# Input projection of a hybrid encoder block: direct products replaced by Strassen's scheme over column pairs

## The chip, the cores and the metric

The kernel runs on 1 core of one Trainium2 chip. The metric is device time in microseconds (us); a profiled execution also gives the span from its first to its last instruction.

## The reference

One encoder layer over 2048 tokens of width 1024, batch 1, float32. What matters here is its first part:

```
h = rmsnorm(x, norm1_g)                     # 2048 x 1024
proj = h @ w_in                             # 1024 x 3264 columns
hq, hi, hf_fwd, hf_bwd, hg = 5 x 512 columns   # recurrence head group
c_q, c_kv, k_r = 384, 256, 64 columns          # latent attention group
y_a = (gla(silu(hq), hi, hf_fwd) + reversed gla(silu(hq), hi, hf_bwd)) normed * silu(hg)
y_b = attention(rmsnorm(c_q) @ w_q_b, rmsnorm(c_kv) @ w_kv_b, rope(k_r))
x = x + concat(y_a, y_b) @ w_out;  x = x + swiglu_ffn(rmsnorm(x));  rmsnorm(x)
```

`gla` is a gated linear recurrence over chunks of 64 tokens, 8 heads of 64; it runs forward in time once and backward in time once.

## The kernel before

Every large product is done in three passes (`mm3`, L191 to L195): each operand is split into a rounded high part and the rest, and high x high, high x low and low x high are summed in PSUM. So each operand tile costs one copy that rounds (often ScalarE) and one subtraction (VectorE or GpSimd). The FFN already works by Strassen's scheme (`slots`, `prods`, `after`); the input projection doesn't.

The part before attention has three stages.

- Stage A (L317 to L367). Token blocks of 512 are normed and transposed (`x_block`); blocks 1 to 3 are prepared as a side channel while products run. Then come the gate columns `hg` (feature-major, `feat_tile`, 128 weights columns against 512 tokens), `hi` as `tp_v` (token-major, 256 columns), `c_q` as `tp_cq` (384) and `c_kv` with `k_r` as `tp_ckv` (320), normed in place and stored.
- Stage B (L586 to L621). For each pair of heads p = 0 to 3 and each block b = 0 to 3, three feature tiles `fp_q`, `fp_f`, `fp_b`, then the elementwise part (`sigmoids`, `decays`: Sigmoid, Ln, scan, Exp) and, as the side channel `ch_f`, the forward part of the recurrence (`rec_block`). The reverse recurrence of p (`back_block`, channel `ch_b`, then `head_norm`) starts when its four blocks are done.
- Stage C (L656 to L788). Latent inputs are loaded back, transposed on TensorE and split (`latent_block`), and projected to keys, values and queries (`tok_proj`, `head_proj`); what is left of the reverse recurrence runs beside it.

Each engine executes its instructions in the order in which they stand; that order comes from the tile framework's scheduler, which keeps near the order of writing. The ticks (`tick`, one after each mm3 of 512 columns) say how far a side channel has got when the next product is written.

## Time and profile before

| | us |
|---|---|
| median of 3 runs | 3129.3 (3118.62 to 3129.41) |
| profiled execution, its own time | 3131.85 |
| its span | 3130.1 |
| TensorE busy in the span | 2985.8 (95%) |
| VectorE, ScalarE, GpSimd busy | 1920.2, 1256.7, 1210.5 |
| stage A, first load to first `fp_q` weights | 0 to 350.6 |
| stage B, to the end of the last `fp_b` | 350.6 to 789.3 |
| stage C, to the first attention scores | 789.3 to 964.8 |

Busy time is the union of an engine's instructions. TensorE's matmuls overlap in the pipeline, so what one costs is read from the distance between starts, and not from its duration. The granted clock was 0.986 of full speed over the span.

### The profile page before, as it was taken

The page shows a single profiled execution, that of the slowest core. Times are in us where ns is not written, and L with a number is a line of the kernel's source. Part 1 is how long each engine was busy: PE and PEld are TensorE (multiplying, and loading weights), DVE is VectorE, ACT ScalarE, POOL GpSimd, SP SyncE. Part 2 cuts the span into 40 slices and gives each one's busy share as a digit, 9 for nine tenths or more (in the row PEclk, how much of TensorE's full clock was granted, in tenths as well). Part 3 has the DMA queues.
Part 4 walks back from the last instruction along what each step waited for, and adds up shares of the span by engine and source line. Part 5 has one row for each costly group of instructions (what it writes and reads, how often), then busy time and mean ns, then how long its engine had stood idle before and what let it go on. Part 6 is the DMA issues. An engine that isn't in the chain of part 4 may idle for free.

```text
span 3130.1 us, 45080 instructions
## 1 busy us (share of the span) xinstructions
PE 2985.8 (95%) x16377; PEld 2491.0 (80%) x16377; DVE 1920.2 (61%) x3986; ACT 1256.7 (40%) x2365; POOL 1210.5 (39%) x1042
## 2 busy tenths in 40 slices
PE   7999999999789999999999999999899999999988
PEld 6899877777677888888877778888688887877776
DVE  6116557787686888888889865555755554432326
ACT  5101366656324555555633333333433333332233
POOL 1110132332333021211023466666566664365652
PEclk9999999999899999999999999999999999999999
DMA  5221112222553010100267543333533332764554
GB/s 178 71 64 57 61 60 83 80 85 81 184 187 131 21 48 28 46 25 19 71 197 227 182 141 100 104 103 101 163 103 101 101 101 100 244 204 139 165 158 154
DMA packets 313758, 349.66 MB, mean 112 GB/s; under 512 B 21016, under 2 KB 221248, under 8 KB 313536
## 3 DMA queue, kind: packets, MB, share of 16 engines
q1 hardware_dynamic: 307840, 339.68, 33.8%
q0 software_dynamic: 4608, 4.20, 0.5%
q8 instruction: 129, 2.11, 0.3%
q10 hardware_dynamic: 1088, 2.90, 0.3%
q14 instruction: 93, 0.76, 0.1%
HBM read 225.07 MB, written 121.63 MB: 111 GB/s over the span
## 4 chain that ended last, share of the span: by engine, by line
PE 58%; DVE 6%; DMA 6%; POOL 3%; issue 2%; ACT 2%; SPq 0%; DVEq 0%; ACTq 0%; POOLq 0%
PE pb L194 4%; PE pb L193 4%; PE pb L195 4%; PE t L885 3%; PE pc L194 2%; PE pa L193 2%; PE pc L195 2%; PE pa L194 2%; PE pa L195 2%; PE pc L193 2%; PE pd_P L194 2%; PE pd_P L195 2%; PE pd_P L193 2%; PE s L852 2%; PE o L193 2%
## 5 line engine op out<-in xcount | busy, mean ns | idle before, releaser
L198 ACT ACTIVATE pth<-t 128x512 fp32r<-128x512 f32 x256 | 153.5, 602 | 250.3 <-PE t L885 250.3
L1264 DVE TENSOR_TENSOR gl_P<-gr_P,gh_P 128x1024 fp32r<-128x1024 f32 x66 | 95.9, 1454 | 239.3 <-ACT gh_P L1263 239.3
L194 PE MATMUL pd_P<-dl_P,gh_P 128*128 128x512 f32 x528 | 208.8, 395 | 16.6 <-POOL dl_P L1255 16.6
L193 PE MATMUL pd_P<-dh_P,gh_P 128*128 128x512 f32 x528 | 207.2, 392 | 5.3 <-DVE t1d L1326 4.1
L859 DVE TENSOR_REDUCE mx<-s 128x1 f32<-128x512 f32 x256 | 175.1, 685 | 56.3 <-PE s L852 56.0
L195 PE MATMUL pd_P<-dh_P,gl_P 128*128 128x512 f32 x528 | 207.5, 393 | 0.0
L868 ACT ACTIVATE pr<-s,nb 128x512 f32<-128x512 f32 x256 | 172.7, 689 | 14.8 <-DVE nb L862 10.9
L199 DVE TENSOR_TENSOR ptl<-t,pth 128x512 fp32r<-128x512 f32 x256 | 174.8, 684 | 2.8 <-ACT pth L198 0.5
L193 PE MATMUL o<-pth,vh 128*128 128x256 f32 x512 | 164.8, 322 | 0.3 <-DVE nb L862 0.3
L885 PEld LDWEIGHTS t<-ident,pr 128*128 128x128 f32 x1024 | 126.5, 141 | 40.5 <-DVE pr L875 1.8
L885 PE MATMUL t<-ident,pr 128*128 128x128 f32 x1024 | 153.9, 273 | 4.4 <-DVE pr L875 3.0
L1263 ACT ACTIVATE gh_P<-gr_P 128x1024 fp32r<-128x1024 f32 x66 | 69.8, 1058 | 203.7 <-PE pd_P L194 181.7
L651 POOL CAST qh<-qraw 128x256 fp32r<-128x256 f32 x31 | 12.4, 400 | 352.7 <-PE s L849 352.6
L195 PE MATMUL o<-pth,vl 128*128 128x256 f32 x512 | 144.0, 281 | 0.0
L194 PE MATMUL o<-ptl,vh 128*128 128x256 f32 x512 | 143.9, 281 | 0.0
L194 PEld LDWEIGHTS pd_P<-dl_P,gh_P 128*128 128x128 f32 x528 | 100.1, 190 | 41.6 <-POOL dl_P L1255 20.7
L1073 DVE TENSOR_TENSOR t<-t,pb 128x512 f32<-128x512 f32 x44 | 30.3, 688 | 162.8 <-PE pb L195 162.8
L875 DVE TENSOR_SCALAR pr<-pr,ri 128x512 f32<-128x512 f32 x256 | 127.7, 513 | 2.2
L193 PEld LDWEIGHTS pd_P<-dh_P,gh_P 128*128 128x128 f32 x528 | 100.3, 190 | 27.1 <-DVE t1d L1326 4.5
L487 POOL TENSOR_TENSOR Am<-az 64x128 f32<-64x128 f32 x64 | 44.1, 690 | 195.5 <-DVE az L484 171.7
L195 PEld LDWEIGHTS pd_P<-dh_P,gl_P 128*128 128x128 f32 x528 | 100.3, 190 | 20.6
L1069 DVE TENSOR_TENSOR U<-t,pb 128x512 f32<-128x512 f32 x44 | 30.2, 686 | 134.2 <-PE pb L195 134.2
(483 smaller groups left out, 9969.2 us busy)
## 6 DMA issues: line engine op xcount, KB each, us to landing
s_gA<-g SPq DMA_DIRECT2D x66, 256.0 KB, 3.2
s_gS<-gS SPq DMA_DIRECT2D x66, 256.0 KB, 2.0
gr_P<-s_gA SPq DMA_DIRECT2D x33, 512.0 KB, 4.2
gr_P<-s_gS SPq DMA_DIRECT2D x33, 512.0 KB, 4.6
B11r<-in_w_gate_dram SPq DMA_DIRECT2D x44, 256.0 KB, 3.9
B12r<-in_w_up_dram SPq DMA_DIRECT2D x44, 256.0 KB, 2.9
B22r<-in_w_up_dram SPq DMA_DIRECT2D x44, 256.0 KB, 2.9
B21r<-in_w_gate_dram SPq DMA_DIRECT2D x44, 256.0 KB, 3.2
```

The lines of the kernel that those rows point to most:

```text
L193: PE.matmul(ps, a_hi, b_hi, start=first, stop=False, skip_group_check=more)
L194: PE.matmul(ps, a_hi, b_lo, start=False, stop=False, skip_group_check=more)
L195: PE.matmul(ps, a_lo, b_hi, start=False, stop=last, skip_group_check=more)
L198: ACT.activation(hi, ps, AF.Copy)
L199: DVE.tensor_tensor(lo, ps, fr(hi), op=ALU.subtract)
L852: PE.matmul(ps, rq[:, qs], rk_lo[b], start=False, stop=True)
L859: last_mx[0] = DVE.tensor_reduce(mx[:, b:b + 1], ps, op=ALU.max, axis=AX.X)
L868: ACT.activation(PR[i][:, b, :], SB[i][b], AF.Exp, scale=SCALE, bias=nb, accum_out=rs[:, b:b + 1])
L875: DVE.tensor_scalar(PR[i][:, b, :], PR[i][:, b, :], ri, None, op0=ALU.mult)
L885: PE.transpose(ps[:, j, :], PR[i][:, b, j * P:(j + 1) * P], ident)
L1263: ACT.activation(hi, raw, AF.Copy)
L1264: DVE.tensor_tensor(lo, raw, fr(hi), op=ALU.subtract)
```

## The change

Everything up to the latent projections is rewritten; attention, output projection and FFN keep their instructions.

- Columns are taken in pairs of 128 (`COLS`): (forward gate, backward gate) and (query, output gate) for each p, three pairs of latent columns (the last pair overlaps, 768 columns for 704), and one pair of 256 for `hi`. Tokens are taken 1024 at a time (two "halves"), rows of w_in in halves of 512. A pair, half and product is 12 matmuls of 512 columns (48 of 256 for `hi`), with 7 products P1 to P7 in place of 8.
- The seven activation operands of half 0 are made on the way in (`x_even`, `x_odd`); those of half 1 are stored to DRAM and split when an operand of half 0 has had its last use (`stage`, `unstage`).
- The sums of weights T1 to T4 are made once by GpSimd and stored to DRAM (`w_sums`); each weight unit is loaded and split for each half anew (`b_load`, `b_make`).
- Products are combined by VectorE (`sums`), and a ScalarE copy takes P1 from PSUM.
- The order is: latent columns and `hi` of half 0, gates and queries of half 0, `hi` of half 1, gates and queries of half 1, latent columns of half 1. The reverse recurrence of p starts when its last block of half 1 is there, beside the remaining products; its scaling of the state moves from VectorE to ScalarE.
- SiLU replaces Sigmoid and a multiplication for `hq` and `hg`.
- Latent inputs are stored feature-major. They are normed after loading: squares, column sums on TensorE, and a product that spreads the factors over partitions; 20 groups of 4 transposes go, 4 groups for `k_r` come.

```diff
-        w = [load_w(wp, w_in[0, :, 2048 + p * P:2176 + p * P], P, f"hg{p}", 3, 4) for p in range(3)]
...
+    main = [(k, p) for p in range(4) for k in ("FB", "QH")]
...
+    islots = [(0, *s) for s in (
+        [(c, pr) for c in (c0, c1, c2) for pr in ("P1", "P2")]
+        + [(c0, "P6"), (c0, "P5"), (c0, "P7"), (c1, "P6"), (c0, "P4"), (c1, "P5"), (c0, "P3"), (c1, "P7"),
...
+        + chain(main)[:-2])]
...
+    islots += [(1, *s) for s in chain(main + [c0, c1, c2])]
...
+    def b_make(m):
+
+        while len(BU) < len(ulist) and len(BU) < ufirst[m] + RING:
+            j = len(BU)
+            if j == len(RAW):
+                b_load(True)
+            BU[j] = hi, lo = [w1.tile([P, 512], F32R, tag=f"w{c}", name=f"w{c}_{j}", bufs=RING) for c in "hl"]
+            ACT.activation(hi, RAW[j], AF.Copy)
+            (DVE if j % 7 in (1, 3, 5) else POOL).tensor_tensor(lo, RAW[j], fr(hi), op=ALU.subtract)
...
+    def x_odd(hf, xs):
+        yield from x_norm(2 * hf + 1, xs)
+        for j in range(4):
+            at = {}
+            for nm, k in (("A21", j), ("A22", j + 4)):
+                ps, g = x_turn(2 * hf + 1, k, xs)
...
+                ACT.activation(at[nm], ps, AF.Copy, scale=g)
...
+            POOL.tensor_tensor(at["S1"], at["A21"], at["A22"], op=ALU.add)
+            DVE.tensor_tensor(at["S3"], A1[j], at["A21"], op=ALU.subtract)
+            POOL.tensor_tensor(at["S2"], at["S1"], A1[j], op=ALU.subtract)
+            POOL.tensor_tensor(at["S4"], A1[j + 4], at["S2"], op=ALU.subtract)
+            if hf == 0:
+                for nm in ("A22", "S3", "S1", "S2", "S4"):
+                    hi, lo = hop[nm]
+                    ACT.activation(hi[:, j, :], at[nm], AF.Copy)
+                    DVE.tensor_tensor(lo[:, j, :], at[nm], fr(hi[:, j, :]), op=ALU.subtract)
...
+            for k in range(4):
+                mm3(ibank[c, key], wu[0][0][:, k, :], wu[0][1][:, k, :], ah[:, k, :], al[:, k, :],
+                    new and k == 0, k == 3, not new)
+                tick()
+            after1(hf, key, pr)
...
+    def sums(get, pr, a, b, c, t1, u2, u3):
+
+        if pr == "P1":
+            ACT.activation(get(t1), a(), AF.Copy)
+        elif pr == "P2":
+            return "C11", a()
+        elif pr == "P6":
+            DVE.tensor_add(get(u2), TM[t1], b())
+        elif pr == "P7":
+            DVE.tensor_add(get(u3), TM[t1], b())
+            DVE.tensor_add(TM[u3], TM[u3], c())
...
+            if d == "F":
+                DVE.tensor_scalar(o[hs, hs], tprev[hs, :], a_in[hs, :], None, op0=ALU.mult)
+            else:
+                ACT.activation(o[hs, hs], tprev[hs, :], AF.Copy, scale=a_in[hs, :])
...
-                for k in range(kt):
-                    ps = rec_tile(f"c{nm}T_{b}_{k}")
-                    for t in range(4):
-                        PE.transpose(ps[:, t * P:(t + 1) * P], src[:, t, k * P:(k + 1) * P], ident)
-                    split_psum(hi[:, k, :], lo[:, k, :], ps)
+                for t in range(4):
+                    PE.matmul(ps[:, t, :], sq[:, k0, t * P:(t + 1) * P], sum1[:, 0:2], start=True, stop=True)
+                r = rstd_of(ps[:, :, 0], 4, dim, f"rc{nm}_{b}")
...
+                R = rec_tile(f"cr{nm}_{b}")
+                PE.matmul(R, sum1, sq[:, k0 + 1, :], start=True, stop=True)
```

The change moves instructions in two places that matter below. The first is TensorE at the start of the program. Before, after the first transposes (`xT`) of token block 0, the products of the gate columns (`fp_hg`) take block 0's operands (`hh_194`, `hl_195`):

```order
L193 MATMUL fp_hg0_0_367<-hh0_194,wh_hg0_0_337 128x512
L193 MATMUL fp_hg1_0_432<-hh0_194,wh_hg1_0_347 128x512
L193 MATMUL fp_hg2_0_517<-hh0_194,wh_hg2_0_357 128x512
L304 MATMUL xT_0_4_301<-ident_74,x_0_0_58 128x128
L304 MATMUL xT_0_4_301<-ident_74,x_0_1_60 128x128
L304 MATMUL xT_0_4_301<-ident_74,x_0_2_62 128x128
L304 MATMUL xT_0_4_301<-ident_74,x_0_3_64 128x128
L194 MATMUL fp_hg0_0_367<-hl0_195,wh_hg0_0_337 128x512
L195 MATMUL fp_hg0_0_367<-hh0_194,wl_hg0_0_338 128x512
```

In the changed kernel six products (P1, P2 of three latent pairs) take block 0's operands; this is the end of them, and what follows:

```order
L201 MATMUL iP1c2_0_721<-hA11h_0_199,wh_4_499 128x512
L202 MATMUL iP1c2_0_721<-hA11l_0_200,wh_4_499 128x512
L203 MATMUL iP1c2_0_721<-hA11h_0_199,wl_4_500 128x512
L201 MATMUL iP6c0_0_817<-hS2h_0_201,wh_6_669 128x512
L201 MATMUL iP5c0_0_870<-hS1h_0_205,wh_7_713 128x512
L202 MATMUL iP5c0_0_870<-hS1l_0_206,wh_7_713 128x512
L203 MATMUL iP5c0_0_870<-hS1h_0_205,wl_7_714 128x512
L202 MATMUL iP6c0_0_817<-hS2l_0_202,wh_6_669 128x512
```

From the fourth of these rows on each product takes an operand (S2, S1) that is made of token blocks 0 and 1.

The second place is ScalarE in the middle of the gate and query products. Before, for p = 1, block 0 (L614 Sigmoid for the query, L401 and L402 Sigmoid for a gate, L410 Ln, L437 and L431 Exp, L485 and L486 copies of the recurrence, L206 an evacuation):

```order
L614 ACT_TABLE_LOAD
L614 ACTIVATE q_1_0_4501<-fp_q1_0_4446 128x512
L206 ACTIVATE kts_0_3_1_4551<-kt_0_3_1_4546 128x512
L401 ACTIVATE A0_1_0_4562<-fp_f1_0_4504 128x512
L402 ACTIVATE N0_1_0_4563<-fp_f1_0_4504 128x512
L410 ACT_TABLE_LOAD
L410 ACTIVATE A0_1_0_4562<-A0_1_0_4562,lb_78,oml_79 128x512
L485 ACTIVATE Am_0_3_0_4582<-G_0_3_0_0_4583 64x2x64
L486 ACTIVATE Am_0_3_0_4582<-G_0_3_0_0_4583 64x2x64
L437 ACT_TABLE_LOAD
L437 ACTIVATE al0_1_4440<-tot0_1_0_4658 128x8
L431 ACTIVATE A0_1_0_4562<-C0_1_0_4657 128x512
```

In the changed kernel, for p = 2 of half 1 (L594 and L596 Sigmoid, L691 Ln, L714 Exp, L667 scaling of the reverse state of p = 0, L358 rounding of a weight unit, L831 squares of the reverse part, L214 an evacuation):

```order
L594 ACT_TABLE_LOAD
L594 ACTIVATE N0_2_2_6151<-iP1FB2_1_5856 128x512
L596 ACTIVATE FB2P2_1_6153<-iP1FB2_1_5856 128x512
L667 ACTIVATE bdB1_1847<-T_B0_8_6169,al1_0_1858 64x64 x2
L691 ACT_TABLE_LOAD
L691 ACTIVATE FB2P2_1_6153<-FB2P2_1_6153,lb_77,oml_78 128x512
L831 ACTIVATE po_0_2_6045<-bo_0_2_5978 128x512
L358 ACTIVATE wh_140_6194<-wr_140_6056 128x512
L214 ACTIVATE kts_1_3_0_6216<-kt_1_3_0_6211 128x512
L667 ACTIVATE bdB0_1846<-T_B0_7_6240,al1_0_1858 64x64 x2
L358 ACTIVATE wh_141_6253<-wr_141_6103 128x512
```

Weight units and the scaling of the reverse state have come between the functions, and each function's table is still loaded anew: over the whole program ScalarE has 130 table loads for 98.

## Rows read from the trace of the kernel before

**Rows 1.** Busy time by stage; columns as named.

```profile
core 0: us, PE busy (x) PEld busy (x) DVE busy (x) ACT busy (x) POOL busy (x), PEclk, DMA share, GB/s
0.00:350.60 350.60, 326.48 (x2049) 304.12 (x2050) 154.18 (x567) 73.66 (x163) 36.60 (x36) 1.00 0.28 89
350.60:789.30 438.70, 422.75 (x3142) 334.09 (x3142) 299.17 (x786) 280.48 (x444) 143.86 (x178) 0.99 0.24 76
789.30:964.80 175.50, 145.75 (x875) 119.60 (x874) 120.56 (x300) 51.40 (x92) 56.42 (x70) 0.91 0.58 202
```

**Rows 2.** Tiles of stage A: duration ns min/median/max, first and last start.

```profile
L193 PE MATMUL fp_hg<-hh,wh_hg x128: 387/389/796, 22.1 to 125.5; 128*128 128x512 f32 x128
...
L193 PE MATMUL tp_v<-wh_v,hh x256: 278/283/284, 126.2 to 218.0; 128*128 128x256 f32 x128
...
L193 PE MATMUL tp_cq<-wh_cq,hh x128: 334/334/339, 218.4 to 285.0; 128*128 128x384 f32 x128
...
L193 PE MATMUL tp_ckv<-wh_ckv,hh x128: 306/309/468, 285.5 to 346.0; 128*128 128x320 f32 x128
```

**Rows 3.** Longest waits of TensorE in stage C: total, times, longest.

```profile
PE ckvT L682 <- DMA ckv<-s_ckv: 5.7, 2, 5.5
PE cqT L682 <- DVE ckvl L199: 5.4, 1, 5.4
```

**Rows 4.** Busy time in two windows of 50 us (stage C, FFN); columns as Rows 1.

```profile
850.00:900.00 50.00, 41.12 (x227) 32.48 (x226) 44.05 (x141) 12.47 (x21) 9.52 (x13) 0.97 0.73 247
1900.00:1950.00 50.00, 50.00 (x219) 40.67 (x218) 22.86 (x27) 15.42 (x27) 30.58 (x22) 1.00 0.33 103
```

**Rows 5.** Timeline of TensorE in stage C: start, duration.

```profile
942.24 0.60 PE L706 MATMUL qrT<-ident,qd 128*128 128x128 f32 x4
942.60 0.48 PE L193 MATMUL kn<-ckvh,wkh 128*128 128x512 f32 x1
```

**Rows 6.** The first transposes and ScalarE reading them; columns as Rows 2.

```profile
L304 PE MATMUL xT<-ident,x x128: 270/273/477, 10.5 to 82.5; 128*128 128x128 f32 x128
L306 ACT ACTIVATE hh<-xT,gcols x32: 679/688/707, 21.4 to 82.9; 128x512 fp32r<-128x512 f32 x32
```

**Rows 7.** Groups of the FFN's Strassen products, 1570 to 3130 us.

```profile
L1076 DVE TENSOR_TENSOR g<-t,U 128x512 f32<-128x512 f32 x44 | 73.2, 1664 | 5.4 <-ACT t L1074 0.7 <-DMA B11d_P<-in_w_down_dram 0.7
...
L1006 POOL TENSOR_TENSOR T<-B12r,B11r 128x512 f32<-128x512 f32 x44 | 57.7, 1312 | 95.4 <-DVE T4l L1022 92.6 <-DMA B12r<-in_w_up_dram 2.6
...
L1022 DVE TENSOR_TENSOR T4l<-T,T4h 128x512 fp32r<-128x512 f32 x44 | 31.2, 709 | 1.9 <-ACT T4h L1020 1.9
...
L1069 DVE TENSOR_TENSOR U<-t,pb 128x512 f32<-128x512 f32 x44 | 30.2, 686 | 134.2 <-PE pb L195 134.2
...
L1020 ACT ACTIVATE B11h<-B11r 128x512 fp32r<-128x512 f32 x44 | 27.8, 632 | 92.9 <-PE pa L194 82.0 <-DMA B11r<-in_w_gate_dram 7.3 <-PE pa L195 2.4
...
L1060 ACT ACTIVATE t<-pa 128x512 f32<-128x512 f32 x44 | 25.5, 579 | 0.2 <-PE pa L195 0.2
```

**Rows 8.** Groups on ScalarE, stage B: count, busy us, mean ns, idle before.

```profile
L410 ACT ACT_TABLE_LOAD x31 | 39.8, 1283 | 0.5
L437 ACT ACT_TABLE_LOAD x31 | 39.8, 1283 | 0.5
...
L401 ACT ACT_TABLE_LOAD x16 | 20.5, 1283 | 0.3
...
L614 ACT ACT_TABLE_LOAD x15 | 19.2, 1283 | 8.2 <-PE fp_q L195 8.1
```

**Rows 9.** Timeline of ScalarE in stage B, around a table load.

```profile
785.75 0.27 ACT L486 ACTIVATE Am<-G 64x128 f32<-64x128 f32 x1
786.04 1.28 ACT L437 ACT_TABLE_LOAD   x1
787.34 0.21 ACT L437 ACTIVATE al<-tot 128x8 f32<-128x8 f32 x1
```

**Rows 10.** Groups on VectorE, stage B.

```profile
L391 DVE TENSOR_SCALAR bdB<-T_B,al 64x64 f32<-64x64 f32 x80 | 28.0, 350 | 4.2 <-PE po L528 3.0
...
L615 DVE TENSOR_TENSOR q<-q,fp_q 128x512 f32<-128x512 f32 x16 | 10.9, 684 | 11.7 <-ACT q L614 11.7
```

More of the change, by code (lines that the diff above doesn't have):

```diff
@@ L96, in drain, with until @@
             tick()
+    def until(pred, *cs):
+        while not pred():
+            assert any(c.queue for c in cs)
+            for c in cs:
+                if c.queue:
+                    c.queue[0][1] = min(c.queue[0][1], clock[0])
+                    c.step()
     def fr(ap):
@@ new lines, in block_kernel, with b_load @@
+    ch_w, ch_f, ch_d, ch_b, ch_n, side = (Channel() for _ in range(6))
+    ulist = [(m, u) for m, (hf, key, pr) in enumerate(islots) for u in range(units(key))]
+    ufirst = {}
+    for j, (m, u) in enumerate(ulist):
+        ufirst.setdefault(m, j)
+    RAW, BU = {}, {}
+    RING, RAWS = 4, 3
+    def b_load(force=False):
+        j = len(RAW)
+        if j >= len(ulist):
+            return False
+        m, u = ulist[j]
+        hf, key, pr = islots[m]
+        nm = B_OF[pr]
+        if nm[0] == "T" and (key, u) not in summed:
+            if not force:
+                return False
+            until(lambda: (key, u) in summed, ch_w)
+        raw = RAW[j] = w1.tile([P, 512], F32, tag="raw", name=f"wr_{j}", bufs=RAWS)
+        if nm[0] == "T":
+            SP.dma_start(out=raw, in_=T_d[nm, key, u])
+        else:
+            SP.dma_start(out=b_view(key, raw), in_=b_src(key, nm, u))
+        return True
@@ new lines, in x_rest, with stage @@
+    def x_rest(xs1):
+        yield from x_odd(0, xs1)
+        for b in (2, 3):
+            xs = x_load(b)
+            yield 4
+            yield from (x_odd if b % 2 else x_even)(1, xs)
+    ibank, TM, decayed, done = {}, {}, set(), set()
+    staged = []
+    order2 = ["A11", "A12", "S2", "S1", "S3", "A22", "S4"]
+    def stage(m):
+        if order2:
+            i = order2.pop(0)
+            raws = [ws_b(j, f"hs_{i}_{j}") for j in range(4)]
+            for j in range(4):
+                SP.dma_start(out=raws[j], in_=h1_d[i][:, j, :])
+            staged.append((m, i, raws))
@@ new lines, in unstage, with hop_switch @@
+    def unstage(m):
+        _, i, raws = staged.pop()
+        hop_tiles(i, 1)
+        hi, lo = hop[i]
+        for j in range(4):
+            ACT.activation(hi[:, j, :], raws[j], AF.Copy)
+            DVE.tensor_tensor(lo[:, j, :], raws[j], fr(hi[:, j, :]), op=ALU.subtract)
+        stage(m)
+    def hop_switch(m):
+        if m == last_use["A11"] - 3:
+            until(lambda: not ch_w.queue, ch_w)
+            stage(m)
+        elif staged and last_use[staged[0][1]] <= m and m >= staged[0][0] + 2:
+            unstage(m)
@@ new lines, in block_kernel, with ws_a @@
+    es_a = ctx.enter_context(ExitStack())
+    stg = es_a.enter_context(pool("stg1"))
+    for _ in range(RAWS):
+        b_load()
+    def ws_a(s, nm):
+        return xpool.tile([P, 512], F32, tag=f"ws{s}", name=nm)
+    first_w = w_sums(c0, 0, ws_a)
+    next(first_w)
+    xs1 = x_load(1)
+    for _ in x_even(0, xs0):
+        pass
+    for _ in first_w:
+        pass
+    for key, u in ((c1, 0), (c2, 0), (v, 0), (v, 1)) + tuple((k, 0) for k in main[:2]):
+        ch_w.add(w_sums(key, u, ws_a))
@@ L369, in block_kernel @@
+    side.add(x_rest(xs1))
+    m1 = 0
+    while islots[m1][1][0] in "cv" or islots[m1][1] not in main:
+        product1(m1)
+        m1 += 1
+    drain(side, ch_w)
+    es_a.close()
     es_x.close()
+    rb = es_b.enter_context(pool("rb", side="right"))
     rec = es_r.enter_context(pool("rec", side="right"))
-    wp = es_l.enter_context(pool("w1b"))
+    tri = rb.tile([P, 2, 2, 64], U8, tag="tri", name="tri")
+    trif = rec.tile([P, 4, P], F32, tag="vb", name="trif", bufs=1)[:, 0:2, :].rearrange("p a (b n) -> p a b n", b=2)
@@ L427, in decays @@
             qk.append((A, C))
+            yield 1
         for d in range(2):
```

561 lines of the change are left out of this document (340 added, 221 removed).

## The prediction

> **What bounds the kernel now.** I read the stages first, since all changed work lies ahead of the first attention scores at 964.8 us. In stages A and B TensorE is busy 326 of 351 us and 423 of 439, while VectorE has 68% and ScalarE 64% of stage B; in stage C TensorE has only 146 of 175.5 [rows 1]. So A and B last as long as TensorE's work, with some 40 us of idle time between them, half of it before the first product at 22.1 us [rows 2]. Stage C also waits: for a reload from DRAM and for the first split operands, 11 us in its two longest waits [rows 3]. Where VectorE is busiest (88% of 50 us, in stage C) TensorE falls to 82% [rows 4]: this is what it looks like when helpers set the pace, though the latent reload plays a part there too.
>
> **The products.** Prices go by the distance of starts. In the FFN window 50 us hold 219 matmuls of 512 columns, 0.228 us each [rows 4]. The 768 matmuls of `tp_v` (256 of each pass) fill the time from 126.2 us to the first of `tp_cq` at 218.4, 0.120 us each; `tp_cq` then lasts to 285.5 (67.1 us) and `tp_ckv` to some 346.5 (61 us) [rows 2]. Before: 384 (`hg`) + 1152 (stage B) matmuls of 512 columns are 350 us, with 92 + 67 + 61 for the others 570 us. After, as the order has them: 11 pairs x 2 halves x 7 products x 12 = 1848 of 512 columns, 421 us, and 672 of 256, 81 us: 502 us. So 68 us of TensorE's work goes.
>
> **Latent operands on TensorE.** 20 groups of four transposes go and 4 come; a group takes 0.36 us (942.24 to 942.60) [rows 5], so 5.8 us goes. What comes is 32 matmuls with 2 columns and 8 with 512 columns of plain f32, neither in the trace at that shape: the first cost from 0 to 0.18 us each (two f32 transposes), the second from 0.23 [rows 4] to 0.72 (twice a group of transposes). That is 2 to 12 us; I take 10, a net of +4 us.
>
> **Stage A after.** To the first product 22 us as before [rows 2], since block 0 goes the same way. Then 252 matmuls of 512 (57.5 us) and 336 of 256 (40.3), the rest of the transposes (24 groups, 8.6), and small waits of 8 (before there were 12: 350.6 - 22.1, less 88 of `hg`, 92, 67, 61 and 8.6). New is a hole. Only the first six products (72 matmuls, 16.4 us) live on block 0; the order shows S1 and S2 right behind. For these, block 1 is normed, transposed and split on ScalarE in four steps of 2 copies at 0.688 [rows 6] and 5 at 0.632 [rows 7], 18 us, with four steps of three GpSimd sums at 1.31 [rows 7] in the same chain. It starts when block 0 is nearly done, so some 18 + 6 us of chain stand against 16 us of products, of which part is spent waiting for block 0 itself. The hole is 0 if the steps interleave perfectly and 24 us if nothing hides it; I take 15, since each step frees a quarter of a product only. Sum: 22 + 57.5 + 40.3 + 8.6 + 8 + 15 = 152 us.
>
> **Stage B after (gates, queries, `hi` of half 1, latent columns of half 1).** TensorE: 1596 matmuls of 512 (1344 + 252), 364 us, 336 of 256, 40 us, and the recurrence's own matmuls, which before were 422.75 - 1152 x 0.228 = 160 us [rows 1]: 564 us.
>
> ScalarE had 280 us here [rows 1]. It gains 34 table loads at 1.283 (127 in this part by the order, for 31 + 31 + 16 + 15 = 93 [rows 8]), 44 us; 147 weight units rounded anew and 28 operand tiles of half 1 at 0.632, 111 us; 21 copies of P1 and 16 more SiLU at 0.579, 21 us [rows 7]; 90 scalings of the reverse state, between 0.21 and 0.27 us by the nearest small activations [rows 9], 22 us. Sum 478 us.
>
> VectorE had 299: 28 us of scalings (`bdB`) and 11 of query products go [rows 10]; 105 sums at 0.686 come (72 us), and 91 low parts from SBUF. Those cost 0.709 at best; at worst 1.66, as the FFN's SBUF product `g` does while GpSimd is busy [rows 7]: 65 to 151 us. I take 80, near the low row, because it is the same form of subtraction. Sum 412 us, at most 483.
>
> So at equal length TensorE has 564, ScalarE 478, VectorE 412 to 483, all in order and each waiting for the others. How long the stage gets is the term that I choose: TensorE's share. It was 0.964 in stage B with helpers at 64 to 68% [rows 1], and 0.82 with one at 88% [rows 4]. At a length of 606 us the helpers stand at 79% and 68 to 80%; this is between, and nearer to the former, so I take 0.93: 564 / 0.93 = 606 us (585 at 0.964, 688 at 0.82). The weights are four units (over 10 us of products) ahead, so a late rounding is hidden; without that cover 1.3 us of each of 147 units would show. DMA had 0.24 of its time here [rows 1]; 147 weight units and the stored sums roughly double this, and the FFN runs at full TensorE with 0.33 [rows 4], so I cost it at nothing.
>
> **Stage C after.** 175.5 us now. +4 us on TensorE; the last forward block, a sixteenth of 160 us, is done before, -8; the chain from the reload to the first operand grows by squares, sums on GpSimd, a column sum, an inverse root and a product. That comes twice with little else to do (block 0, block 2), as the waits of 5.7 and 5.4 us show [rows 3]. It is 0 if the reverse recurrence of p = 3, which still reaches into this stage, fills it, and 20 if not; I take 8. Sum 179 us.
>
> **Sum.** 152 + 606 + 179 = 937 us for 964.8, so 28 us less. Against the profiled execution's own 3131.85 that is 3104; the median of the runs shown is 2.5 us below that execution, so the time I name is 3102 us. A change of under 0.5% (15.6 us) can hardly be told from none with this kernel.
>
> **Rivals.**
> - *TensorE stays the bound.* The helpers' queues are long enough; share 0.964 in stage B (585 us), hole 5 (142), latent chain hidden (171): 898 us, 67 less, 3062. For it: in stage B ScalarE's idle time is mostly waiting for TensorE's results, such as the 8.1 us ahead of a load [rows 8], so it has room. Against: three engines above 70% have not run at once in the trace.
> - *Nothing is gained.* Hole 20 and share 0.90 (627): 157 + 627 + 181 = 965 us, 3129. For it: the 68 us saved are only 12% of stages that already lose 40.
> - *ScalarE sets the pace; slower.* If it can't be kept busy for more than 71% of the time, because Ln waits for sigmoids, Exp for scans and each late one blocks weights and P1 copies queued behind it, stage B is 478 / 0.71 = 673 us, the sum 1004 and the time 3169. It decides from a ScalarE share below 0.75 on (478 / 0.75 = 637, where nothing is left of the gain). For it: 64% is all that stage B shows [rows 1]. Against: nothing pressed it there.
> - *A switch of tables costs more than its row.* If each of 127 switches stopped ScalarE for two loads' length, it had 478 + 127 x 1.28 = 641 us, more than TensorE, and the sum would be 152 + 641 + 179 = 972: 3137. The rows speak against it: the load starts at 786.04, the copy before ends at 786.02, and the next function starts at 787.34, 1.30 us in all [rows 9]. The Trainium skill, "ScalarE: Activation LUTs", section "What ACT_TABLE_LOAD costs", gives 1283 ns for the load and some 1380 ns of drain on top at every switch, and would have this rival come true. The trace agrees with its first figure and shows no such drain around the load.
>
> VectorE's upper price is no rival of its own (483 us is still below TensorE). The Trainium skill, "GPSIMD Engine Reference", section "Specifications", says that GpSimd shares its SBUF interfaces with VectorE, to the cost of VectorE instructions with two SBUF inputs. The FFN rows agree: 1664 ns for `g` from two SBUF tiles, 686 for a sum with a PSUM input.
>
> **How the numbers follow.** Forecast (3085 to 3120) 0.38, TensorE-bound 0.22, nothing gained 0.22, ScalarE-bound 0.14, table switches 0.04. Faster by over 0.5% (below 3114): 0.33 of the forecast, 0.22, 0.03 of the third: 0.58. Within 0.5%: 0.05 + 0.16 + 0.03 = 0.24. Slower: 0.03 + 0.14 + 0.01 = 0.18. The range leaves out about half of the TensorE-bound case's low end and the upper half of the ScalarE-bound one: 3055 to 3160; the forecast's own is 3085 to 3120.
>
> **What would show it.** In the profile after: first product near 22 us and a gap on TensorE in the 25 us behind the sixth product, ended by the high or low parts of S1 to S4; first FB product at about 152 us; about 606 us from there to the last product of the latent columns, with ScalarE near 79% busy and 127 loads at 1.28; 512-column matmuls still 0.23 us apart where dense; first scores at about 937 us. I am wrong if the stage between is shorter than 585 or longer than 640 us, if TensorE's waits there are mainly for DMA (weights, stored sums) instead of ScalarE and VectorE, or if stage C moves by more than 15 us.

## The result: 3239.6 us, slower by 3.6 per cent

The changed kernel takes 3239.6 us (median of 4 runs, 3221.4 to 3242.6), the kernel before 3124.7 us (4 runs, 3118.6 to 3129.4). The ratio is 1.0357, with a 95% interval of 1.0311 to 1.0402. The forecast was 3102 us, the range 3055 to 3160: wrong, and on the wrong side.

The profiled execution has a span of 3240.1 us. The first product starts at 26.5 us, the first FB product at 205.4, the last product of the latent columns ends at 883.9, and the first attention scores start at 1078.0. From there to the end it is 2162 us, as before (964.8 to the end: 2165). So all of the loss lies in the three stages that were forecast, and these are their windows in the profile after; the columns are those of [rows 1].

```profile
core 0: us, PE busy (x) PEld busy (x) DVE busy (x) ACT busy (x) POOL busy (x), PEclk, DMA share, GB/s
0.00:205.40 205.40, 140.86 (x718) 114.71 (x719) 110.09 (x211) 77.62 (x132) 112.81 (x87) 0.88 0.72 230
205.40:883.90 678.50, 623.25 (x4120) 501.20 (x4118) 438.88 (x933) 483.87 (x812) 254.94 (x268) 0.93 0.47 143
883.90:1078.00 194.10, 143.44 (x696) 112.59 (x696) 123.83 (x338) 60.24 (x100) 63.63 (x68) 0.83 0.49 169
```

How to read them: length less TensorE's busy time is its idle time, 64.5 + 55.3 + 50.7 = 170.5 us, for 24.1 + 16.0 + 29.8 = 69.8 before [rows 1]. PEclk is the granted share of the clock, 0.5 or 1.0 at any one time (1.2 or 2.4 GHz). Busy time times (1 - PEclk) is roughly what the lower level costs: 16.9 + 43.6 + 24.4 = 85 us, for 0 + 4 + 13 = 17 before. The rest is TensorE's work at full clock: 1078.0 - 170.5 - 85 = 823 us, for 964.8 - 69.8 - 17 = 878. So the change did save work, 55 us of it. It lost 101 us to waiting and 68 us to the clock; less the 55, that is the 113 us more until the first scores. (Counted by the records that lie in a stretch at the lower level, the clock's part is 17 + 46 + 15 = 78 us, for 13 before: the rough figure is too high in the third stage, where TensorE often stood during such a stretch.)

What ends TensorE's waits, by stage (total, times, longest), from the list of waits of the three windows:

```profile
PE xT L383 <- DVE x L372: 12.0, 5, 4.7
PE iP5c L201 <- ACT hS1h L419: 9.5, 3, 6.1
PE pg L153 <- DMA grows<-in_lb_logits_dram: 8.5, 1, 8.5
PE iP6c L201 <- DVE c2P L508: 6.7, 1, 6.7
...
PE kt L742 <- DVE C L721: 10.4, 3, 5.0
PE o L791 <- POOL Am L780: 9.6, 13, 3.1
PE u L750 <- DVE kts L216: 9.0, 6, 3.5
...
PE iP6QH L203 <- POOL wl L359: 5.7, 1, 5.7
...
PE crq L965 <- DVE sq L961: 14.5, 2, 10.4
PE krT L991 <- POOL kd L941: 7.1, 3, 5.6
PE cskv L957 <- POOL sq L952: 6.3, 2, 5.3
...
PE crkv L965 <- DVE rcq_r L196: 4.7, 1, 4.7
```

No single engine stands out. In the first stage it is mostly the operands of block 1 (`pg` is the first load of the program), in the second the recurrence (`kt`, `u`, `o`) and one low part of a weight, in the third the norm of the latent inputs. None of the longest waits of the second stage is for DMA, though its share doubled from 0.24 [rows 1] to 0.47.

The hole behind the sixth product is there: in the 30 us from 57 to 87 TensorE does the 24 matmuls of two products and 8 transposes. It idles for 15.1 us of them, which is what was forecast, and the clock stood at 0.59, which no term had. Timelines of GpSimd, ScalarE and VectorE in its middle (start, duration):

```profile
67.24 1.27 POOL L412 TENSOR_TENSOR s<-a,a 128x512 f32<-128x512 f32 x1 [1.90 <-ACT a L409]
69.32 1.65 POOL L414 TENSOR_TENSOR a<-s,a 128x512 f32<-128x512 f32 x1 [0.80 <-DVE a L413]
71.05 1.60 POOL L415 TENSOR_TENSOR a<-a,a 128x512 f32<-128x512 f32 x1
72.60 6.42 POOL L315 TENSOR_TENSOR ws_c<-ws_c,ws_c 128x512 f32<-128x512 f32 x4
78.97 1.26 POOL L412 TENSOR_TENSOR s<-a,a 128x512 f32<-128x512 f32 x1
...
75.39 0.62 ACT L419 ACTIVATE hA22h<-a 128x512 fp32r<-128x512 f32 x1
81.00 0.63 ACT L419 ACTIVATE hS3h<-a 128x512 fp32r<-128x512 f32 x1 [4.98 <-DVE a L413]
...
80.27 0.69 DVE L413 TENSOR_TENSOR a<-a,a 128x512 f32<-128x512 f32 x1 [3.71 <-POOL s L412]
```

S1, S2 and S4 (L412, L414, L415) stand one behind the other, and then a set of weight sums (L315, four subtractions, 6.42 us) comes in front of the next S1. S3 on VectorE (L413), which overwrites an input of S1, waits 3.71 us for that S1, and ScalarE waits 4.98 us for S3, with the high parts of S1 and S2 queued behind.

The clock falls behind single stalls. Windows around one in the second stage, and the row of TensorE's timeline that ends it:

```profile
444.00:456.00 12.00, 12.00 (x90) 10.53 (x88) 10.84 (x18) 10.45 (x17) 5.46 (x4) 1.00 0.54 167
456.00:458.20 2.20, 0.09 (x1) 0.00 (x0) 2.15 (x7) 2.20 (x5) 0.09 (x1) 1.00 0.32 119
458.30:468.30 10.00, 10.00 (x67) 7.79 (x68) 6.36 (x12) 6.88 (x14) 3.45 (x5) 0.50 0.63 185
468.60:480.00 11.40, 11.32 (x103) 10.13 (x102) 7.98 (x14) 9.23 (x20) 7.28 (x8) 1.00 0.47 138
```

```profile
458.26 1.09 PE L742 MATMUL kt<-ident,C 128*128 128x128 f32 x4 [2.17 <-DVE C L721]
```

TensorE was fully busy for 12 us, stood for 2.17 us, and was fully busy again for 10 us at half the clock. The stall itself costs 2.2 us and the 10 us behind it about 5. The second stage has 11 such falls, 3.4 to 13.7 us long, 95.6 us in all, and ahead of each stands a stall of 1.9 to 5.7 us. In stage B of before [rows 1] no stall was that long, and the lower level held for 6.8 us, at its start, behind a stall of 4.0 us at the end of stage A. Not every fall has such a stall ahead of it: in stage A of before the lower level held for 3.4 us from 289.7 us on, with no stall over 0.6 us in the 12 us ahead.

### The profile page after: what moved, and what is told of

Its sections match the earlier page's. It is cut to its first block, busy times and chain, and to the rows that moved or that the text cites. A ratio compares the mean times of both kernels' runs of the same rounds, so it can differ in the third digit from the quotient of the medians.

```text
span 3240.1 us, 44914 instructions
## 1 busy us (share of the span) xinstructions
PE 2995.5 (92%) x15841; PEld 2462.8 (76%) x15841; DVE 2017.9 (62%) x3815; ACT 1474.4 (46%) x2711; POOL 1404.1 (43%) x1182
## 3 DMA queue, kind: packets, MB, share of 16 engines
q8 instruction: 125, 2.05, 0.3%
## 4 chain that ended last, share of the span: by engine, by line
PE 49%; DMA 5%; DVE 5%; POOL 4%; issue 4%; ACT 1%; SPq 0%; DVEq 0%; POOLq 0%; ACTq 0%
PE pb L202 3%; PE pb L203 3%; PE pb L201 3%; PE t L1180 3%; PE pc L203 2%; PE pc L202 2%; PE pa L201 2%; PE pc L201 2%; PE pa L202 2%; PE pa L203 2%; POOL dl_P L1545 2%; PE o L201 2%; PE o L202 2%; PE s L1145 2%; PE o L203 2%
## 5 line engine op out<-in xcount | busy, mean ns | idle before, releaser
L206 ACT ACTIVATE pth<-t 128x512 fp32r<-128x512 f32 x256 | 153.8, 603 | 241.1 <-PE t L1180 241.0
L359 POOL TENSOR_TENSOR wl<-wr,wh 128x512 fp32r<-128x512 f32 x104 | 140.0, 1348 | 235.7 <-ACT wh L358 210.7
L1553 ACT ACTIVATE gh_P<-gr_P 128x1024 fp32r<-128x1024 f32 x66 | 69.8, 1058 | 205.6 <-PE pd_P L202 181.8
L358 ACT ACTIVATE wh<-wr 128x512 fp32r<-128x512 f32 x182 | 112.6, 625 | 109.0 <-PE iP6v L203 15.2
```

Source lines behind the costliest of these rows:

```text
L206: ACT.activation(hi, ps, AF.Copy)
L358: ACT.activation(hi, RAW[j], AF.Copy)
L359: (DVE if j % 7 in (1, 3, 5) else POOL).tensor_tensor(lo, RAW[j], fr(hi), op=ALU.subtract)
```

## The experiments

All times are medians of 4 executions (10 for x9) beside runs of the kernel before on the same chip. Stages A, B and C end with the first FB product, the last product and the first scores in the profile. What comes after the first scores is the same work in all of them and took 2150 to 2167 us, so the last column is the sharper measure where few us matter.

| kernel | us | ratio to before (95%) | stage A | stage B | stage C | first scores |
|---|---|---|---|---|---|---|
| before (its own stages) | 3124.7 | 1 | 350.6 | 438.7 | 175.5 | 964.8 |
| changed | 3239.6 | 1.0357 (1.0311-1.0402) | 205.4 | 678.5 | 194.1 | 1078.0 |
| x1 zeros in the waits | 3234.0 | 1.0349 (1.0334-1.0365) | 204.8 | 672.3 | 196.9 | 1074.0 |
| x2 no table switches | 3204.8 | 1.0258 (1.0240-1.0277) | 204.7 | 650.7 | 194.7 | 1050.0 |
| x3 no weight sums | 3178.5 | 1.0169 (1.0154-1.0185) | 167.3 | 652.5 | 196.4 | 1016.2 |
| x4 operand sums on VectorE | 3229.3 | 1.0330 (1.0315-1.0346) | 199.1 | 670.2 | 196.1 | 1065.4 |
| x5 = x2 + x3 | 3163.3 | 1.0118 (1.0103-1.0133) | 168.0 | 630.5 | 194.7 | 993.2 |
| x6 no subtractions | 3194.3 | 1.0219 (1.0202-1.0237) | 183.6 | 652.3 | 196.0 | 1031.9 |
| x7 stores by GpSimd | 3243.8 | 1.0366 (1.0345-1.0388) | 212.3 | 678.2 | 194.8 | 1085.3 |
| x8 no latent norm | 3192.0 | 1.0216 (1.0197-1.0235) | 204.9 | 675.8 | 151.0 | 1031.8 |
| x9 = x2 + x3 + x8 | 3118.9 | 0.9974 (0.9961-0.9986) | 166.6 | 638.8 | 152.1 | 957.6 |
| x10 weight sums on VectorE | 3206.3 | 1.0260 (1.0243-1.0278) | 187.9 | 657.2 | 194.8 | 1039.9 |
| x11 low parts on VectorE | 3204.3 | 1.0253 (1.0227-1.0280) | 196.0 | 651.0 | 195.8 | 1042.7 |
| x12 first repair | 3193.0 | 1.0225 (1.0200-1.0250) | 180.7 | 654.0 | 195.4 | 1030.1 |
| x13 all repairs | 3153.1 | 1.0085 (1.0055-1.0115) | 174.1 | 638.4 | 184.4 | 996.9 |
| x14 a third of the zeros | 3223.4 | 1.0307 (1.0282-1.0331) | 206.8 | 670.0 | 195.9 | 1072.7 |
| x15 x11 + idle GpSimd work | 3314.7 | 1.0601 (1.0558-1.0644) | 309.6 | 645.6 | 196.1 | 1151.3 |
| x16 the same, tied to units | 3213.9 | 1.0280 (1.0250-1.0310) | 200.1 | 658.0 | 195.7 | 1053.8 |
| x17 x13 + more on VectorE | 3164.8 | 1.0119 (1.0092-1.0147) | 177.6 | 638.5 | 182.6 | 998.7 |

**x1: is it the waits that bring the clock down?**

```diff
+    PE.matmul(WB[0], zr, zr.unsqueeze(1).to_broadcast([P, 4, P]), start=new and i == 0, stop=False, ...)
+            at("kt")                       # n zeros here, by a table of the longest waits
             pt = rec_tile(f"kt_{p}_{b}_{d}")
```

> The changed kernel with some 370 matmuls of zeros (512 columns, added into the bank that TensorE is working on, or into a free one) just ahead of the places where TensorE waited longest in the first 1078 us, about as many at each place as the wait is long. The output stays the same. Theory: the falls of the granted clock (212 us of the first 1078 at the lower level, against 41 us in the kernel before) come from TensorE standing still, so with the waits filled the time at the lower level falls below 100 us and the kernel gets 40 to 80 us faster than the changed one: 3160 to 3200 us. Rival: the clock falls for another reason (load of the whole chip, DMA); then the time at the lower level stays near 200 us and the kernel is at 3240 or up to 60 us above it, since zeros cost up to 80 us where they don't fall into a wait.

```profile
204.80:877.00 672.20, 629.95 (x4294) 491.82 (x4293) 435.56 (x933) 476.79 (x806) 252.64 (x268) 0.98 0.46 143
877.00:1074.00 197.00, 175.49 (x887) 125.17 (x886) 123.17 (x337) 60.08 (x100) 64.10 (x68) 0.97 0.48 166
```

With the zeros in, the granted clock goes from 0.93 to 0.98 in the second stage and from 0.83 to 0.97 in the third, so it does follow TensorE's standing still: until the first scores the lower level held for 75 us instead of 212. But the time hardly moves, and the 40 to 80 us that the theory gave it did not come. In the third stage TensorE is 32 us busier and the stage no shorter. Either its chain does not run on TensorE, so that a faster TensorE only waits longer, or the zeros ran on beyond the waits that they were to fill; x1 does not separate the two. In the second stage the zeros took about what the clock gave. What the clock is worth there is better read from x2, below.

**x2: does ScalarE set the pace?** SiLU, Ln and Exp (L600, L606, L691, L714 to L717) become Sigmoid.

```diff
-            ACT.activation(A, A, AF.Ln, scale=oml[:, d, p:p + 1], bias=lb[:, d, p:p + 1])
+            ACT.activation(A, A, AF.Sigmoid, scale=oml[:, d, p:p + 1], bias=lb[:, d, p:p + 1])
```

> The changed kernel with Sigmoid in place of SiLU, Ln and Exp in the input projection and the recurrence (so what these compute is changed), which takes the 127 loads of a table out of the part from 205 to 888 us, 163 us of ScalarE's 487 busy us. Theory of several chains that wait for each other: ScalarE is one link of several, and the stage gets 10 to 35 us shorter. Rival 'ScalarE sets the pace': with a third of its work gone the stage falls to TensorE's own 580 us, so 80 to 100 us less: 3140 to 3160 us. If ScalarE is never the link: under 8 us.

```profile
204.70:855.40 650.70, 597.57 (x4120) 482.99 (x4118) 440.76 (x933) 324.86 (x686) 250.30 (x268) 0.97 0.49 149
```

ScalarE loses 159 of its 484 us and the stage only 28 of 678 (the other 7 of the 35 us lie behind the first scores, in work that was not changed). So ScalarE is one link among several, and does not set the pace. TensorE's idle time falls by no more than 2 us (55.3 to 53.1); its busy time falls by 26 at the same 4120 instructions, since the clock stands at 0.97 for 0.93: the lower level held for 44 us instead of 96. Here the clock is nearly the whole gain.

**x3, x6, x7: what the sums of weights cost.** x3 leaves them out; x6 leaves out only the subtractions; x7 has GpSimd issue the stores.

```diff
-            SP.dma_start(out=raw, in_=T_d[nm, key, u])                 # x3: the plain block instead, no w_sums
-            POOL.tensor_tensor(t[d], t[a], t[b], op=ALU.subtract)      # x6
-            SP.dma_start(out=T_d[nm, key, u], in_=t[d])                # x7
+            POOL.dma_start(out=T_d[nm, key, u], in_=t[d])
```

> The changed kernel without the sums of weights: in place of T1 to T4 the products take B11, B22, B12 and B21 straight from the weights (so the products are no longer Strassen's), and the 13 sets of four loads, four subtractions on GpSimd (6.4 us a set) and four stores are gone. Theory: in the first 205 us these sums stand ahead of the operand sums on GpSimd and of the loads in SyncE's queue, and part of the hole of the first 90 us and the late first product (26.5 for 22.1 us) are theirs: 10 to 25 us less, nearly all of it before the first FB product. Rival 'DMA is the bound of the first 300 us' (0.72 busy): 13 x 12 transfers of 256 KB, of which 8 in 12 go, some 20 MB of 47 in the first stage, and 40 us or more go with them. If neither: under 5 us.

> The changed kernel without the four subtractions of each of the 13 sets of weight sums on GpSimd (6.4 us a set, 83 us); the loads, the stores and the loads of T through DRAM stay, so T1 to T4 are plain weight blocks. If the 61 us of the sums are a matter of GpSimd's time and of what waits behind it there and behind the stores in SyncE's queue, most of it goes here: 3185 to 3200 us. If they are the price of the transfers (the DMA queues 0.72 busy in the first 205 us), nearly nothing goes: 3225 to 3240 us.

> The changed kernel with the stores of T1 to T4 issued by GpSimd, which has just made them, in place of SyncE, whose queue waited 43 us in the first 205 us on these stores and on what they store; the output stays the same. If SyncE's queue is the link (loads of weights and of x stand behind stores that wait for GpSimd), 15 to 40 us go: 3200 to 3225 us. If GpSimd's time or the transfers themselves are the price, there is no change or a few us more, since the issues now take GpSimd's time: 3235 to 3250 us.

x3: 61 us, 38 in the first stage and 26 in the second, far beyond the 10 to 25 expected, and within what the DMA rival named. x6 decides between them, as the transfers stay in it: it gives 45 of the 61 us. So three quarters are GpSimd's 52 subtractions, and the remaining 16, all in the first stage, go with the transfers. x7 gives nothing. It took the waits at these stores (L319, 38 us; the expectation has 43) out of SyncE's queue in the first stage, but other waits came in their place (139 us in all for 116), and GpSimd, which now issues the stores, is 21 us busier there; so it shows that this exchange doesn't pay, and not what SyncE's queue cost by itself.

**x4: the hole's chain.** S1, S2 and S4 go to VectorE (`POOL.tensor_tensor` to `DVE.tensor_tensor` at L412, L414, L415), the low parts of A22 and S3 to GpSimd.

> The changed kernel with the three operand sums S1, S2, S4 of the first half on VectorE (0.69 us each) in place of GpSimd (1.28, 1.65 and 1.60 us), and the low parts of A22 and S3 on GpSimd in exchange. Theory: the hole between 57 and 87 us is this chain, four steps of 7.3 us of which 4.5 us are GpSimd's sums one behind the other, with one set of weight sums in between (6.4 us): each step loses about 2 us, the fourth its wait behind the weight sums, so 8 to 14 us less until the first FB product, and 3226 to 3232 us in all. Rival: the hole is set by the loads of block 1 and of the weights: no change.

10 us, 6 of them before the first FB product, where 8 to 14 were expected: the chain is a link as read, but a small part of the 53 us by which that stage missed its forecast.

**x8: the latent norm.** No squares, column sums, inverse roots or product with them.

```diff
-                    DVE.scalar_tensor_tensor(a, a, g, R, op0=ALU.mult, op1=ALU.mult)
+                    DVE.tensor_scalar(a, a, g, None, op0=ALU.mult)
```

> The changed kernel without the norm of the latent inputs behind their reload: no squares, no sums, no column sums, no inverse roots and no product with them, only the gain and the two parts. The stage from the last product to the first scores took 194 us (110 us of TensorE's work, 51 us idle, 65 us at the lower clock level, which is some 33 us lost). Theory: the chain of the norm is the longest wait of that stage (crq, cskv, crkv: 33 us idle) and brings the clock down with it, so 30 to 45 us go: 3195 to 3210 us. My forecast had 8 us for it (0 to 20): then 3220 to 3235 us.

The stage falls from 194.1 to 151.0 us, and the time by 48. Of the 43 us, 24 are TensorE's busy time (143.4 to 119.5), which are the norm's own matmuls, and 19 are idle time (50.7 to 31.6). I had put in 10 and 8 for these two.

**x5 and x9: do the costs add up?**

> Both of the earlier cuts in one kernel: no sums of weights (the products take plain weight blocks) and Sigmoid for SiLU, Ln and Exp in the projection and the recurrence (no table loads). Alone they gave 61 and 35 us against the changed kernel's 3239.6. If they are separate costs, 96 us go together: 3140 to 3150 us. If both only shorten the same waits (TensorE at the end of one shared chain), the two overlap by 20 us or more: 3160 to 3175 us. Stage 205 to 884 us by itself: 575 us of TensorE's own work, so at most 50 us more than that is left in it.

> The three earlier cuts in one kernel: no sums of weights (plain weight blocks as T1 to T4), Sigmoid for SiLU, Ln and Exp, no norm of the latent inputs. The first two together gave 76 us, the third alone 48. The stages are apart in time, so if the costs are apart too the kernel is at 3239.6 - 76 - 48 = 3115 us (3108 to 3125), 12 us below the kernel before: with its three side costs taken out for nothing the change is worth about half a per cent. If the 68 us saved on the products were all still there behind these costs, it would be at 3060 to 3080.

x5 gives 76 us where the two alone gave 61 and 35, but until the first scores it is 85 of 62 + 28: they are almost wholly separate, and the difference lies in the unchanged work behind. x9 lands at 3118.9 as its first theory had it. Even with weight sums, table switches and latent norm taken out for nothing, the change is worth 0.26% (0.14 to 0.39).

```profile
0.00:166.60 166.60, 130.05 (x717) 108.05 (x718) 97.48 (x211) 77.97 (x132) 69.72 (x55) 0.93 0.60 193
166.60:805.50 638.90, 600.55 (x4120) 486.90 (x4118) 432.83 (x933) 324.74 (x686) 220.90 (x248) 0.96 0.45 133
805.50:957.60 152.10, 119.82 (x617) 97.81 (x617) 88.70 (x209) 49.86 (x92) 48.68 (x56) 0.90 0.63 216
```

By the reckoning of the result section TensorE idles 107 us in it and loses 45 to the clock, 152 together for 87 before. Its work at full clock is some 72 us less than before, of which the norm's matmuls, left out here, are a part; 65 of those go into the additional waiting and clock.

**x10, x11, x13: GpSimd's work to VectorE.** x10 moves the weight sums, x11 the low parts of the weights, x13 both, with the operand sums, and gives the diagonal of the latent norm to ScalarE.

```diff
-            POOL.tensor_tensor(t[d], t[a], t[b], op=ALU.subtract)
+            DVE.tensor_tensor(t[d], t[a], t[b], op=ALU.subtract)
-            (DVE if j % 7 in (1, 3, 5) else POOL).tensor_tensor(lo, RAW[j], fr(hi), op=ALU.subtract)
+            DVE.tensor_tensor(lo, RAW[j], fr(hi), op=ALU.subtract)
-                    DVE.tensor_scalar(dg[:, t, :], ident, r[:, t:t + 1], None, op0=ALU.mult)
+                    ACT.activation(dg[:, t, :], ident, AF.Copy, scale=r[:, t:t + 1])
```

> The changed kernel with the four subtractions of each set of weight sums on VectorE in place of GpSimd; the output stays the same. Theory: GpSimd's 6.4 us sets hold up what waits behind them on GpSimd and lengthen VectorE's own instructions meanwhile (VectorE's instructions that overlap GpSimd's took 78 us over their usual time between 205 and 884 us), and on VectorE a set takes 4 x 0.69 = 2.8 us, 36 us in all: most of the 45 us of the kernel without these subtractions, so 3200 to 3215 us. Rival: it is the work as such, on whichever engine: VectorE pays 36 us in a stage where it has 65%, and the time is 3225 to 3245.

> The changed kernel with the low parts of all weight units on VectorE (0.69 us) in place of four in seven on GpSimd (1.3 us, some 100 of them). Theory that GpSimd's instructions on SBUF hold VectorE up: GpSimd loses some 130 us of work, VectorE gets 70 us more but loses much of its 112 us of lengthening before 884 us, and the kernel is 5 to 25 us faster: 3215 to 3235 us. Rival: VectorE's queue is the tighter one, and 70 us more in it cost time: 3245 to 3270 us.

> All repairs in one, output unchanged: weight sums, operand sums and the low parts of all weight units on VectorE, the diagonal of the latent norm by ScalarE. Alone the moves gave 33 (weight sums), 35 (low parts) and 10 us (operand sums). If they are separate costs: 3155 to 3170 us. If they shorten the same waits or VectorE becomes the tight queue (some 100 us more work on it before 884 us): 3185 to 3205 us.

33 and 35 us each, and 86 together with the operand sums and the diagonal (until the first scores 38, 35 and 81): these costs nearly add up, so VectorE was not the tight queue. x11 and x13 both gave somewhat more than their first theories expected. x13 is 2.7% faster than the changed kernel, and still 0.85% (0.55 to 1.15) slower than the kernel before.

**x12 and x17: repairs that went too far.** x12 has the weight and operand sums on VectorE and, in the norm, the diagonal on ScalarE and the squares added up by TensorE; x17 is x13 with the additions of the squares and of the rotated halves on VectorE.

> Three repairs in one, the output unchanged: the weight sums and the operand sums S1, S2, S4 on VectorE; in the norm of the latent inputs the diagonal by ScalarE (it took VectorE 7.64 us for four 128 x 128 products while GpSimd made low parts, and 0.87 us for the four before), and the squares added up by TensorE's accumulation instead of GpSimd's additions (4.3 us in block 0). If the costs are where the runs so far put them: 25 to 40 us from the sums, 8 from the operand sums, 8 to 15 from the norm: 3180 to 3200 us. If they only shift the wait to the next link: 3215 to 3235.

> The kernel with all repairs (3153 us), and the additions of the squares of the latent inputs and those of the rotated keys and queries on VectorE too; the output stays the same. These GpSimd additions end 20 us of TensorE's waits in its last stage of 184 us (cskv, csq, krT, qrT) and take about half as long on VectorE, and the clock gains with the stalls: 3138 to 3150 us. If VectorE only takes the wait over: 3150 to 3158.

x12's third stage stays at 195.4 us, where x13's is 184.4: TensorE idles 17 us less in it (33.7 for 50.7), and is busy for 18 us more, with the squares that it adds up. x17 is not better than x13 (1.0119 for 1.0085, the intervals just overlapping; 182.6 for 184.4 in its third stage): VectorE took the wait over, as `krT` now waits 8.4 us for VectorE's additions and waited 8.1 for GpSimd's in x13.

**x14: a third of the zeros.**

> The changed kernel with 75 matmuls of zeros, a third of the first number and only up to 884 us, so some 18 us of them, placed ahead of the longest waits; the output stays the same. Theory: it is the long stalls that bring the clock down; broken up they leave less time at the lower level (147 us up to 884 us now, then 80 or less), worth 33 us at half price, for at most 10 us of zeros that don't fall into a wait: 3215 to 3230 us. Rival: what is won at the clock is lost at the next wait, as with all the zeros: 3234 to 3245 us.

3223.4, in the range of the theory, but its interval overlaps that of the changed kernel. The second stage is 8.5 us shorter (670.0) with the lower level at 61 us instead of 96, in both stages together 113 instead of 147, where the theory had 80 or less; nothing can be said beyond "some of it can be had".

**x15 and x16: late results, or GpSimd in VectorE's way?** x11 plus four subtractions on GpSimd for each unit taken from it, whose result nobody reads.

```diff
+                    POOL.tensor_tensor(junk2, ident[:, 0:64], ident[:, 64:128], op=ALU.subtract)              # x15
+                    POOL.tensor_tensor(junk2, fr(hi[:, 0:64]), fr(hi[:, 64:128]), op=ALU.subtract)            # x16
```

> The kernel with the low parts of all weight units on VectorE (3204 us), and GpSimd given four subtractions of 128 x 64 from constants for each of the units that it lost, about as long together, whose result nobody reads; the output stays the same. If GpSimd's lateness was the cost (products and stores waiting for its low parts), nothing changes: 3200 to 3212 us. If its instructions hold VectorE up by being there, most of the 35 us is lost again: 3225 to 3245 us.

> The kernel with the low parts of all weight units on VectorE (3204 us), and GpSimd given four subtractions of 128 x 64 for each of the units that it lost, from the unit's high part, about as long together, whose result nobody reads; the output stays the same. If the lateness of GpSimd's low parts was the cost, little changes: 3200 to 3215 us. If it is GpSimd's work as such, lengthening VectorE's instructions and standing ahead of its own sums, most of the 35 us is lost again: 3225 to 3245 us.

x15 doesn't answer the question. Its work depends on nothing and was placed first: GpSimd is busy for 233 us in a first stage of 310, with the operand and weight sums late behind it. It shows only what late sums cost. In x16 the work lies where the low parts lay. GpSimd is busier than in the changed kernel (124 + 296 for 113 + 255 us), yet only 10 of the 35 us come back, at intervals that overlap. So GpSimd's busy time as such was not the price. But x16 can't tell late low parts from long VectorE instructions. Up to the last product, x11 gave VectorE 104 low parts more, 72 us at 0.69, and its busy time rose by 26 only (549 to 575 us), so some 46 us of lengthening were gone; x16, whose GpSimd instructions take 0.46 us each where a low part took 1.35, puts only 14 of these back. For the other cause speaks that TensorE's waits for GpSimd's low parts, 13.4 us in the changed kernel, are gone in x11 (one of 9.7 us for a high part has come in their place). How the 35 us divide stays open.

## Why the prediction was wrong, step by step

**Products: right.** 512-column matmuls are 0.23 us apart where dense (454.31 to 455.70 us: six steps), as forecast. The work saved on TensorE comes out at some 55 us, after the latent operands and other small work.

**Latent operands on TensorE: mis-sized.** The column sums took 0.95 to 1.87 us for a group of four, the broadcast products 1.02 to 2.05 us each; 8 groups and 8 products are 24 us of TensorE's busy time, part of it at the lower clock, where I took 10 and had 12 as the upper end.

**Stage A, 152 forecast, 205 measured.** The first product came at 26.5 instead of 22.1. The hole was read rightly (block 1's chain, parts of S1 to S4), and its 15.1 us of idle time are the 15 that I took, in part by luck, since a set of weight sums (6.42 us) stands in it. What I left out is these sums: the 52 subtractions stand in no term of the sum, and on GpSimd they take 72 us (the 83 of the expectations put one set's 6.4 us for each of the 13), 45 of them in this stage (112.8 us busy, 67.9 without them in x6), in the same queue as the operand sums and the low parts. They cost 38 us here with their transfers (x3), 16 of them the transfers (x6 against x3): DMA had no term in this stage either. Some 17 us of this stage are lower clock, for which there was no term at all. Without the weight sums it still takes 167 us (x3). GpSimd's time was in fact summed in no stage: it went from 36.6 and 143.9 us busy in the first two [rows 1] to 112.8 and 254.9.

**Stage B, 606 forecast, 678.5 measured.** TensorE's own work was nearly right: 623 busy, less 44 for the clock, is 580 for 564. VectorE's 439 lie between the 412 and 483 that I had. ScalarE's sum was right as well: 484 busy for 478, 127 loads at 1283 ns, of which these are two groups:

```profile
L594 ACT ACT_TABLE_LOAD x28 | 35.9, 1283 | 0.5
L691 ACT ACT_TABLE_LOAD x28 | 35.9, 1283 | 0.5
```

The step that failed is TensorE's share of 0.93. It came out at 0.919 busy, so close to it, and the stage was still 72 us longer, because the share has no clock in it: 44 us of those 623 are the lower level. The 72 us are these 44, 16 by which TensorE's work came out above 564, and 13 more of waiting (55 for the 42 that 606 less 564 had). Stage B of [rows 1] could not show the clock's part, since it had no stall long enough, but stage C there did: 29.8 us of idle time beside a clock of 0.91. The share should have been split into short waits, which cost their length, and single stalls, which cost about twice theirs: the 12 stalls of over 1.8 us in this stage are 39 us together. Also, "a late rounding is hidden" by units that are four ahead failed for the low parts: TensorE waited 7.7 us of this stage for GpSimd's, one wait of 5.7 us among them.

**Stage C, 179 forecast, 194 measured.** The terms for the latent norm were 10 us of TensorE's time and 8 of waiting (0 to 20); their cost is 24 and 19, together 43 (x8). The waiting is within its bounds and the matmuls are not. The rows named the chain, but I took its links at their usual price and let the reverse recurrence fill it; 10.4 us of the waiting is one wait that is told below.

**The signs.** Of the three signs of being wrong that the prediction named, two came: the second stage took longer than 640 us, and stage C moved by 18.6 us (175.5 to 194.1). The third, waits mainly for DMA, did not.

**The rivals.** "ScalarE sets the pace" gave 673 us for this stage at a ScalarE share of 0.71, and the profile shows 678.5 and 0.713. By the numbers it came true, by its mechanism not: with ScalarE's share cut to 0.50 the stage is still 651 us (x2). "A switch costs more than its row" is out: what idles ahead of 28 loads is 0.5 us in all, so the drain that the Trainium skill, "ScalarE: Activation LUTs", section "What ACT_TABLE_LOAD costs", states does not show here either. The rival that was missing is that each stall of TensorE costs its clock too. The Trainium skill, "TensorE: Matmul & The Clock Gate", section "HAM oscillation — how this bites in real kernels", describes a kernel whose waits bring the clock down again and again, and prices the time at the lower level at half of it. The trace agrees (10 us at 0.50 behind 2.17 us of waiting), and I had not weighed it.

What stays open: the first stage of x13 is still 22 us above its forecast. The second stage of x9 and x13 still has 38 us of waits and a clock of 0.96 to 0.97, and no run took the recurrence's own waits (`u`, `o`, `kt`) away. What the clock costs by itself was bounded, not measured: x1 and x14 pay for it with other work.

## What to carry to other kernels

A change that saves 12% of TensorE's work in a stage by giving every helper more to do has to be priced by queue: list for each engine everything that is put in front of what TensorE waits for next, sums made ahead of time included. Price a stall of TensorE at its length plus half of the time at the lower clock that the rows show behind such stalls, which here about doubled it. And before moving work to the engine that has most idle time, ask what is queued behind it there, and what it holds up elsewhere: most of 86 us came back by taking three small jobs from GpSimd, which was only 43% busy.

## What the runs showed of the hardware

A short VectorE instruction can be held until a GpSimd instruction on SBUF ends. Timelines of VectorE and GpSimd in the third stage of the changed kernel, and the durations of the last four VectorE instructions one by one (ns, shortest/median/longest):

```profile
894.90 2.31 DVE L188 TENSOR_TENSOR rckv_t<-rckv_t,rckv_a 128x4 f32<-128x4 f32 x1
898.71 0.87 DVE L961 TENSOR_SCALAR sq<-ident,rckv_r 128x128 f32<-128x128 f32 x4
904.39 7.64 DVE L961 TENSOR_SCALAR sq<-ident,rcq_r 128x128 f32<-128x128 f32 x4
...
894.85 2.34 POOL L915 TENSOR_TENSOR wkl<-wkr,wkh 128x1024 fp32r<-128x1024 f32 x1 [0.42 <-ACT wkh L914]
904.31 2.35 POOL L915 TENSOR_TENSOR wkl<-wkr,wkh 128x1024 fp32r<-128x1024 f32 x1 [7.12 <-ACT wkh L914]
906.63 5.31 POOL L915 TENSOR_TENSOR wql<-wqr,wqh 128x768 fp32r<-128x768 f32 x3
...
L961 DVE TENSOR_SCALAR sq<-ident,rcq_r x4: 1836/1838/2361, 904.4 to 910.2; 128x128 f32<-128x128 f32 x4
```

Four instructions of one form took 0.87 us with GpSimd idle and 7.64 us beside it. Beside it the first took 2.36 us and each of the others 1.84, and GpSimd's four took 2.35 us and three times 1.79: each VectorE instruction ended 0.08 us after one of GpSimd's, so one got through for each of them. A 128 x 4 product of 0.16 us took 2.31 and ended with GpSimd's too. The 7.64 us are most of the 10.4 us wait of `crq`, and with the diagonal on ScalarE the third stage is 10 us shorter (x13; 194.1 to 184.4). The Trainium skill, "GPSIMD Engine Reference", section "Specifications", names such contention for VectorE's two-port modes and for two SBUF inputs. The trace agrees for the product of two SBUF tiles (2.31 us for 0.16); in which mode the four instructions with one SBUF tile ran, no run here shows. The size follows from the rows: what these VectorE instructions lost went by the length of the GpSimd instruction beside them, and not by their own. What this cost over the first two stages stays open (x16).
